# A hybrid decoder step on one core: value tiles turned by VectorE and DMA, copies and loads moved, two buffers for the last blocks

## The chip, the cores and the metric

The kernel runs on one core of one Trainium2 chip. The metric is the device time of one launch in microseconds (us), the median of several runs.

## The reference

One inference step of a one-layer decoder trunk, for 256 prompt tokens and 32 sample tokens (8 sequences of 4), 288 together. Width is 2048, everything is float32.

```
x = x + 1/2 * post1(SwiGLU_1(pre1(x)))
x = x + post2(HybridMixer(pre2(x)))
x = x + 1/2 * post3(SwiGLU_2(pre3(x)))

proj = h @ w_in                                  # q, k, v, a_lr, r | hq, hf, hi, hg
S_t  = diag(exp(log_a_t)) S_{t-1} + k_t^T v_t    # per head, causal
o_t  = q_t S_t                                   # token t reads its own update
out  = concat(rmsnorm(o) * silu(gate)) @ w_out
```

All `pre` and `post` are RMS norms. Each SwiGLU has a hidden width of 5632. The mixer has 4 GLA heads (keys of 128, values of 256) and 8 HGRN heads (128 and 128). The prompt starts with a zero state; each sample sequence brings its own. The outputs are x and the new states.

## The kernel before

**Layout.** Activations lie with features on the 128 partitions and the 288 tokens along the free dimension, in 16 tiles `x[k]` and 16 tiles `y[k]`. Columns 0 to 255 are the prompt, 256 to 287 the samples.

**Matmuls.** A weight unit is 128x1024 numbers, loaded by the SP queue into one of three `raw` buffers (L61, L63). ScalarE rounds it to `wh` (L95) and VectorE makes the remainder `wl` (L96), into one of four buffers. Each product is three matmuls (L520 to L522): `xh*wh`, `xl*wh`, `xh*wl`. A `block` is four output tiles in four PSUM banks of the `mm` pool (five banks): for each k, twelve matmuls, then a call of `tick(k)`. At the block's end `evac(f, ps)` empties each tile. Three more banks are the `aux` pool, for everything else.

**The mixer.** Blocks in order: qk0, v0, qk1, v1, hfq0, hi0, hfq1, hi1, hfq2, hfq3, four gates, then the output projection. A block of values (v0, v1, hi0, hi1) gives four tiles. The scan of a head pair is a generator; every `tick` runs one step of it between two k of a block, and pops one closure from the list `turns` (not at k = 0). The scan's steps 0 to 8 build the causal matrices `Dg` and `Ds` level by level: `put01` places levels 0 and 1 with masked copies (L937, L939, L945, L950), `lay23` prepares the operands of levels 2 and 3 (L976, L977), `score23` multiplies them (L983), `put23` places them (L994). Then `key_t` turns the keys, `out` (L1113 to L1117) multiplies the values by `Dg` and `Ds`, `final` makes the prompt's state (L1126), and `sample` updates and stores the samples' states (L1163, L1165). `load_state` (L895) loads those states, in steps 5 to 8 and on later need.

**Turning the values.** Products come with features on partitions, but the scan's stationary operand needs tokens there. For every tile `ev_v` multiplies by the norm's factor (L849 for the prompt; L850 writes the sample columns three times into `v3`). Its `turn` then makes three PE transposes into one bank (L828 twice, L829) and ScalarE and VectorE copy out the prompt part (`Vt`, L857), the samples (`V32`, L858) and a stacked hi/lo form of the samples (`Vs`, L833 and L835).

**The end.** In the second SwiGLU, x is turned during four earlier output blocks and z (the scaled output) during the last four. `turn32` makes VectorE transposes of 32x32 blocks into `b32` (L625) and `bs32` (L627); after four tiles `move32` moves the blocks to their places by 20 DMAs (L636, L640), for x from POOL, for z alternately from POOL and SP. There is one pair `b32`, `bs32`. The last group of z is turned by PE (`by_token`, L646). `finish` adds and stores.

**Order.** Tile's scheduler lays down each engine's instruction order from the program's order and its own estimate of when operands are ready; `tc.issue_after(ins)` keeps an instruction behind another one on the same engine.

Of the kernel before, what the change touches and what calls it, by code (L numbers as in the profile page):

```python
# [37 lines left out]
class Weights:  # L38


    def __init__(self, tc, rawp, hlp):
        self.tc, self.nc, self.rawp, self.hlp = tc, tc.nc, rawp, hlp
        self.srcs, self.raws, self.parts = [], {}, {}
        self.loaded = self.split = self.used = 0
        self.extra, self.extra_units = None, ()
        self.behind = None
# [8 lines left out]
    def load(self):  # L55
        i, src = self.loaded, self.srcs[self.loaded]
        raw = self.rawp.tile([P, 1024], F32, name=f"raw{i}", tag="raw")
        if isinstance(src, list):
            for c, part in src:
                w = part.shape[2]  # L60
                self.nc.sync.dma_start(raw.rearrange("p (a b) -> p a b", b=512)[:, :, c:c + w], part)  # L61
        else:
            self.nc.sync.dma_start(raw.rearrange("p (a b) -> p a b", b=src.shape[2]), src)  # L63
        self.raws[i] = raw
        self.loaded += 1
# [59 lines left out]
def trunk_kernel(ctx, tc, x_prompt, x_sample, state_gla, state_hgrn, norm_gains, f1_in, f1_out, f2_in, f2_out,  # L125
# [115 lines left out]
    y = [xpool.tile([P, T], F32, name=f"y{k}") for k in range(KT)]  # L241
# [324 lines left out]
    def ffn(tag, gcol, gnext, pn, before, fill=None):  # L566
# [3 lines left out]
        with ExitStack() as pools:  # L570
# [43 lines left out]
            lasts, zs = [], []  # L614

            def last_pool():

                zp = pools.enter_context(tc.tile_pool(name="last", bufs=1, side="right", reuse_waits="tile"))
                for n in ("z", "x"):
                    final_tiles.append((zp.tile([P, KT, 2, P], F32, name=f"{n}T"), zp.tile([P, D // 4], F32, name=f"{n}S")))  # L620

                final_tiles.append((zp.tile([P, 4, 8, TS], F32, name="b32"), zp.tile([P, 4, TS], F32, name="bs32")))

            def turn32(src, f):
                V.transpose(final_tiles[2][0][:, :, 2 * f:2 * f + 2, :],  # L625
                            src[:, 0:TP].rearrange("p (t q c) -> p q t c", t=2, q=4))
                V.transpose(final_tiles[2][1][:, f, :], src[:, TP:T])  # L627

            def move32(g, dst, dsts, queues):

                b32, bs32 = final_tiles[2]
                n = 0
                for b in range(4):
                    rows, cols = slice(b * TS, (b + 1) * TS), slice(b * TS, (b + 1) * TS)
                    for q in range(4):
                        queues[n % len(queues)].dma_start(  # L636
                            dst[q * TS:(q + 1) * TS, 4 * g:4 * g + 4, :, cols].rearrange("p k t c -> p (k t) c"),
                            b32[rows, q])
# [17 lines left out]
            def do_out(c, n):  # L656
# [8 lines left out]
                for o in range(4):  # L665
                    def ev(f, ps):
# [74 lines left out]
    def mixer(pn, border):  # L741
        with ExitStack() as mx:
# [82 lines left out]
            def by_token(tp, src, src3):  # L825

                for t in range(2):
                    PE.transpose(tp[:, t * P:(t + 1) * P], src[:, t * P:(t + 1) * P], ident)  # L828
                PE.transpose(tp[0:96, TP:TP + P], src3, ident)  # L829
# [7 lines left out]
            def vtiles(nm):  # L837
                vs32.append(vs32.pop(0))
                return (gp.tile([P, 2, 512], F32, name=f"V{nm}", tag="V"), vs32[-1],
# [4 lines left out]
            def ev_v(Vt, V32, Vs, y0=8):  # L844
                def ev(f, ps):

                    vt = y[y0 + f]
                    v3 = tmp.tile([P, 3, TS], F32, name="v3", tag="v3", bufs=4)
                    V.tensor_tensor(vt[:, 0:TP], ps[:, 0:TP], rt[:, 0:TP], op=ALU.mult)  # L849
                    V.tensor_tensor(v3, ps[:, TP:T].unsqueeze(1).broadcast_to([P, 3, TS]),  # L850
                                    rt[:, TP:T].unsqueeze(1).broadcast_to([P, 3, TS]), op=ALU.mult)

                    def turn():
                        tp = auxtile("tp_v")
                        by_token(tp, vt, v3.rearrange("p n t -> p (n t)"))
                        c = slice(f * P, (f + 1) * P)
                        S.activation(Vt[:, 0:2, c], tp[:, 0:TP].rearrange("p (t c) -> p t c", c=P), AF.Copy)  # L857
                        S.activation(V32[0:TS, c], tp[0:TS, TP:TP + P], AF.Copy)  # L858
                        stack(Vs[:, c], tp, TS)

                    turns.append(turn)
                return ev
# [9 lines left out]
            def scan(d, Vt, V32, Vs, gla, ytile0, s0, sp_out, ss_out):  # L872
# [56 lines left out]
                def put01(ps, po):  # L929
# [3 lines left out]
                    v = Dflat.rearrange("p (i a) (n two) -> p i a n two", a=2, two=2)  # L933
                    ov = po[:, 0:T].rearrange("p (a c) -> p a c", a=2)
                    sv = Ds[0:TS].rearrange("p a (n two) -> p a n two", two=2)
                    for i in range(2):
                        V.copy_predicated(v[:, i, :, :, 0], eye(P, 64).unsqueeze(1).broadcast_to([P, 2, 64]),  # L937
                                          ov[:, :, i * 64:(i + 1) * 64])
                    V.copy_predicated(sv[:, :, :, 0], eye(TS, 16).unsqueeze(1).broadcast_to([TS, 2, 16]),  # L939
                                      ov[0:TS, :, P:])  # L940
                    for lv in range(2):
                        h = 1 << lv
                        m = mk[:, lv * 64:(lv + 1) * 64]
                        dst = Dflat.rearrange("p j (n two k) -> p j n two k", two=2, k=h)[:, :, :, 1, :]
                        V.copy_predicated(dst, m.rearrange("p (n k) -> p n k", k=h).unsqueeze(1).broadcast_to(dst.shape),  # L945
                                          ps.rearrange("p (j l n k) -> p j l n k", j=4, l=2, k=h)[:, :, lv])
                        dst = Ds[0:TS].rearrange("p a (n two k) -> p a n two k", two=2, k=h)[:, :, :, 1, :]
                        for a in range(2):
                            c = T + a * TS + lv * 16
                            V.copy_predicated(dst[:, a], m[0:TS, 0:16].rearrange("p (n k) -> p n k", k=h),  # L950
                                              po[0:TS, c:c + 16].rearrange("p (n k) -> p n k", k=h))
# [16 lines left out]
                def lay23(part):  # L968
# [7 lines left out]
                    V.tensor_tensor(far, src, f.broadcast_to(src.shape), op=ALU.mult)  # L976
                    S.activation(near, src, AF.Copy)  # L977

                def score23():
                    pss = [auxtile(f"sc23_{i}") for i in range(2)]  # L980
# [61 lines left out]
                for step in range(LEVELS + 1):  # L1042
# [14 lines left out]
                    elif step == 3:  # L1057
                        put01(*pss.pop(1))
                        update(2, False)
                        lay23(1)  # L1060
                    else:
# [7 lines left out]
                        update(step - 1)  # L1069
                    if step == 3:  # L1070
# [35 lines left out]
                def out(a):  # L1106
                    vc = Vt[:, :, a * dv:(a + 1) * dv]

                    po, ss = auxtile("o"), auxtile("os")
                    for j in range(nv):  # L1110
                        vj = vc[:, :, j * P:(j + 1) * P]
# [9 lines left out]
                def final(a):  # L1121

                    kd, vc = kds[a][0], Vt[:, :, a * dv:(a + 1) * dv]
                    ps = auxtile("st")
                    for t in range(2):
                        PE.matmul(ps[:, 0:dv], kd[:, t, :], vc[:, t, :], start=t == 0, stop=t == 1)  # L1126
# [203 lines left out]
            for g in range(2):  # L1330
# [5 lines left out]
                if g == 0:  # L1336
                    vt = vtiles("g0")
                    block("v0", KT, xrhs, ev_v(*vt), 
# [3 lines left out]
                else:  # L1342
                    gla_decay(d, g)
                    vt = vtiles("g1")
                    block("v1", KT, xrhs, ev_v(*vt), tick=tick)
# [3 lines left out]
            for kind, g in HORDER:  # L1349
                if kind == "hi":  # L1350
                    written(g)
                    vts[g] = vtiles(f"h{g}")
                    block(f"hi{g}", KT, xrhs, ev_v(*vts[g], 8 + 4 * g), tick=tick)
# [4 lines left out]
                for j in list(ds):  # L1358
                    if j // 2 in vts:
                        c = slice((j % 2) * 256, (j % 2 + 1) * 256)  # L1360
                        vt, v32, vs = vts[j // 2]
                        gens.append((2 + j, scan(ds.pop(j), vt[:, :, c], v32[:, c], vs[:, c], False, 8 + 2 * j,
# [114 lines left out]
```

## Time and profile before

| | |
|---|---|
| median of 3 runs | 2280.1 us (2279.67 to 2280.32) |
| the profiled execution: time | 2280.79 us |
| its span | 2279.0 us |
| granted TensorE clock, mean | 0.999 |
| busy: PE, DVE, ACT, POOL | 2264.1, 1420.8, 1034.4, 115.8 us |
| DMA | 382.42 MB, mean 168 GB/s |

PE is TensorE, PEld its weight loads, DVE VectorE, ACT ScalarE, POOL GpSimd, SP the sync engine that issues most DMAs. Busy times are shares of the span. Matmuls are pipelined, so the duration of one is longer than the distance to the next one; for what a matmul costs, read the distance between starts. A wait in square brackets in a timeline is idle time before the instruction, with what ended it.

### The profile page before, as it was taken

How to read it: one execution, taken by the hardware profiler on the slowest of the kernel's cores; microseconds unless marked ns; L12 is line 12 of the kernel's file. 1: busy time of each engine (PE TensorE's matmuls, PEld its weight loads, DVE VectorE, ACT ScalarE, POOL GpSimd, SP SyncE). 2: the span in 40 equal slices, each digit the busy share in tenths (PEclk: the TensorE clock that was granted, in tenths of full speed). 3: DMA queues.
4: the chain of work that ended last, by engine and by line, in shares of the span. 5: the costliest groups of instructions: out<-in, count | busy, mean ns of one | idle time of the engine just before them, and what ended most of it. 6: DMA issues, size and time to landing. Idle time of an engine off the chain costs nothing.

```text
span 2279.0 us, 42090 instructions
## 1 busy us (share of the span) xinstructions
PE 2264.1 (99%) x17164; PEld 2252.0 (99%) x17164; DVE 1420.8 (62%) x2375; ACT 1034.4 (45%) x1603; POOL 115.8 (5%) x204
## 2 busy tenths in 40 slices
PE   9999999999999999999999999999999999999998
PEld 9999999999999999999999999999999999999997
DVE  7545545554555468889889754954555455545546
ACT  6443333333334346556656654644333333333344
POOL 0000000000000002001000000260000000000003
PEclk9999999999999999999999999999999999999999
DMA  7555555555555545456465554475555555555555
GB/s 218 169 165 165 165 167 165 166 166 167 167 167 185 166 158 163 139 171 198 144 183 159 167 183 160 141 203 169 165 166 164 166 167 166 167 167 167 167 163 151
DMA packets 228801, 382.42 MB, mean 168 GB/s; under 512 B 24018, under 2 KB 63936, under 8 KB 228608
## 3 DMA queue, kind: packets, MB, share of 16 engines
q1 hardware_dynamic: 219088, 366.27, 50.7%
q0 software_dynamic: 7344, 13.29, 2.1%
q8 instruction: 134, 2.20, 0.4%
q10 hardware_dynamic: 2176, 0.18, 0.1%
q14 instruction: 59, 0.48, 0.1%
HBM read 363.75 MB, written 11.80 MB: 165 GB/s over the span
## 4 chain that ended last, share of the span: by engine, by line
PE 94%; DVE 3%; DMA 1%; ACT 1%; issue 0%; DVEq 0%; SPq 0%; ACTq 0%
PE gate L522 9%; PE gate L520 9%; PE gate L521 9%; PE up L522 8%; PE up L520 8%; PE up L521 8%; PE out L521 8%; PE out L522 8%; PE out L520 8%; PE hfq L520 2%; PE hfq L522 2%; PE mo L522 1%; PE mo L520 1%; PE mo L521 1%; PE hfq L521 1%; PE v L520 1%
## 5 line engine op out<-in xcount | busy, mean ns | idle before, releaser
L96 DVE TENSOR_TENSOR wl<-raw,wh 128x1024 fp32r<-128x1024 f32 (+1 forms) x674 | 821.6, 1219 | 621.0 <-ACT wh L95 619.1
L95 ACT ACTIVATE wh<-raw 128x1024 fp32r<-128x1024 f32 (+1 forms) x674 | 711.6, 1057 | 1017.6 <-PE gate L521 315.8
L522 PE MATMUL gate<-xh,wl 128*128 128x288 f32 x1660 | 489.0, 295 | 0.2 <-DVE wl L96 0.2
L520 PE MATMUL gate<-xh,wh 128*128 128x288 f32 x1660 | 488.9, 296 | 0.3 <-ACT wh L95 0.3
L521 PE MATMUL gate<-xl,wh 128*128 128x288 f32 x1660 | 485.5, 295 | 0.0
L522 PE MATMUL out<-hh,wl 128*128 128x288 f32 x1408 | 415.1, 295 | 0.9 <-DVE wl L96 0.9
L521 PE MATMUL out<-hl,wh 128*128 128x288 f32 x1408 | 415.7, 295 | 0.0
L522 PE MATMUL up<-xh,wl 128*128 128x288 f32 x1408 | 415.0, 295 | 0.0
L520 PE MATMUL up<-xh,wh 128*128 128x288 f32 x1408 | 414.8, 295 | 0.1
L521 PE MATMUL up<-xl,wh 128*128 128x288 f32 x1408 | 414.6, 294 | 0.0
L520 PE MATMUL out<-hh,wh 128*128 128x288 f32 x1408 | 413.7, 294 | 0.0
L522 PEld LDWEIGHTS gate<-xh,wl 128*128 128x128 f32 x1660 | 311.5, 188 | 0.6 <-DVE wl L96 0.6
L520 PEld LDWEIGHTS gate<-xh,wh 128*128 128x128 f32 x1660 | 310.9, 188 | 1.2 <-ACT wh L95 0.5
L521 PEld LDWEIGHTS gate<-xl,wh 128*128 128x128 f32 x1660 | 310.4, 188 | 0.2
L522 PEld LDWEIGHTS out<-hh,wl 128*128 128x128 f32 x1408 | 264.7, 188 | 1.1 <-DVE wl L96 1.1
L520 PEld LDWEIGHTS out<-hh,wh 128*128 128x128 f32 x1408 | 264.6, 188 | 0.0
L520 PEld LDWEIGHTS up<-xh,wh 128*128 128x128 f32 x1408 | 264.1, 188 | 0.5 <-ACT g L590 0.3
L521 PEld LDWEIGHTS out<-hl,wh 128*128 128x128 f32 x1408 | 264.4, 188 | 0.0
L521 PEld LDWEIGHTS up<-xl,wh 128*128 128x128 f32 x1408 | 264.2, 188 | 0.1
L522 PEld LDWEIGHTS up<-xh,wl 128*128 128x128 f32 x1408 | 264.2, 188 | 0.0
L671 DVE TENSOR_TENSOR y<-out,y 128x288 f32<-128x288 f32 x288 | 121.4, 452 | 98.9 <-PE out L522 95.9
L520 PE MATMUL hfq<-xh,wh 128*128 128x288 f32 x256 | 77.5, 303 | 0.0
(381 smaller groups left out, 2598.2 us busy)
## 6 DMA issues: line engine op xcount, KB each, us to landing
raw<-in_ffn_w_in_dram SPq DMA_DIRECT2D x351, 512.0 KB, 3.4
raw<-in_ffn_w_out_dram SPq DMA_DIRECT2D x176, 512.0 KB, 3.5
raw<-in_mix_w_in_dram SPq DMA_DIRECT2D x64, 512.0 KB, 3.7
raw<-in_mix_w_in_dram SPq DMA_DIRECT2D x96, 256.0 KB, 3.2
raw<-in_mix_w_out_dram SPq DMA_DIRECT2D x32, 512.0 KB, 3.7
out_dram<-s POOLq DMA_DIRECT2D x32, 256.0 KB, 3.5
s<-in_state_gla_dram SPq DMA_DIRECT2D x16, 256.0 KB, 4.2
s<-in_state_hgrn_dram SPq DMA_DIRECT2D x16, 256.0 KB, 3.6
```

Source lines behind the costliest of these rows:

```text
L95: i1 = self.nc.scalar.activation(h[:, c], raw[:, c], AF.Copy).ins
L96: i2 = self.nc.vector.tensor_tensor(l[:, c], raw[:, c], h[:, c].bitcast(F32), op=ALU.subtract).ins
L520: yield lambda: PE.matmul(dst, w[0][:, c:c + P], parts[0], start=start, stop=False)
L521: yield lambda: PE.matmul(dst, w[0][:, c:c + P], parts[1], start=False, stop=False)
L522: yield lambda: PE.matmul(dst, w[1][:, c:c + P], parts[0], start=False, stop=stop)
L671: V.tensor_tensor(y[k], ps, y[k], op=ALU.add)
```

## The change

Five edits:

1. `put01` does only the odd masked copies (L945) in step 3 and returns two closures, the even ones and the samples' ones, which run after `lay23`, one in step 3 and one at the end of the next steps. `lay23` issues its ScalarE copy ahead of its VectorE product. The second tile of `score23` comes from the `mm` pool.
2. `load_state` is kept behind the load of the weight unit three before the newest.
3. `b32` and `bs32` have two buffers. For the first two groups of z all moves are issued by POOL; for the third by POOL and SP.
4. `y` is four tiles of four. `ev_v` makes one product of 288 columns. In v0, v1 and hi0 the turns are: two steps of VectorE 32x32 transposes, two tiles a step (the blocks lie in a spare group of `y`), four steps of moves by POOL (16 DMAs of blocks, and with the first step 4 of samples), one empty step. hi1 keeps PE's transposes.
5. In all four blocks the stacked form `Vs` is made from `V32` for four tiles at once (`parts`: two copies of 32x512 on ScalarE, one subtraction on VectorE). `Vt` is laid out by tile, and `out` and `final` index it so.

```diff
-                    pss = [auxtile(f"sc23_{i}") for i in range(2)]
+                    pss = [auxtile("sc23_0"), mmtile("sc23_1")]
...
-                        put01(*pss.pop(1))
+                        puts = put01(*pss.pop(1))
                         update(2, False)
-                        lay23(1)
+                        ready = lay23(1)
+                        with tc.issue_after(ready):
+                            puts.pop(0)()
...
                         update(step - 1)
+                        if puts:
+                            with tc.issue_after(ready):
+                                puts.pop(0)()
...
-                        nc.sync.dma_start(t, s0[b0:b0 + nb, a].rearrange("b p v -> p b v"))
+                        with tc.issue_after(W.last[W.loaded - 3]):
+                            nc.sync.dma_start(t, s0[b0:b0 + nb, a].rearrange("b p v -> p b v"))
...
-                final_tiles.append((zp.tile([P, 4, 8, TS], F32, name="b32"), zp.tile([P, 4, TS], F32, name="bs32")))
+            def blocks32():
+                zp = final_tiles[2]
+                return (zp.tile([P, 4, 8, TS], F32, name="b32", tag="b32", bufs=2),
+                        zp.tile([P, 4, TS], F32, name="bs32", tag="bs32", bufs=2))
...
-                                        move32(o, *zt, (G, nc.sync))
+                                        move32(o, *zt, (G, nc.sync) if o == 2 else (G,))
...
+                def turn32(f):
+                    def run():
+                        for i in (f, f + 1):
+                            V.transpose(b32[:, :, 2 * i:2 * i + 2, :], vg[:, i, 0:TP].rearrange("p (t q c) -> p q t c", t=2, q=4))
+                        if f:
+                            V.transpose(bs32, vg[:, :, TP:T])
+                    return run
+                def move32(b, sample):
+                    rows = cols = slice(b * TS, (b + 1) * TS)
+                    def run():
+                        if sample:
+                            for n in range(4):
+                                r = slice(n * TS, (n + 1) * TS)
+                                G.dma_start(V32[0:TS].rearrange("p (f c) -> p f c", c=P)[:, :, r], bs32[r])
+                        for q in range(4):
+                            G.dma_start(Vt[q * TS:(q + 1) * TS, :, :, cols].rearrange("p f t c -> p (f t) c"), b32[rows, q])
+                    return run
+                def parts():
+                    v = V32[0:TS, :]
+                    S.activation(Vs[0:TS, :], v, AF.Copy)
+                    V.tensor_tensor(Vs[TS:2 * TS, :], v, Vs[0:TS, :].bitcast(F32), op=ALU.subtract)
+                    S.activation(Vs[2 * TS:96, :], v, AF.Copy)
                 def ev(f, ps):
-                    V.tensor_tensor(vt[:, 0:TP], ps[:, 0:TP], rt[:, 0:TP], op=ALU.mult)
-                    V.tensor_tensor(v3, ps[:, TP:T].unsqueeze(1).broadcast_to([P, 3, TS]),
-                                    rt[:, TP:T].unsqueeze(1).broadcast_to([P, 3, TS]), op=ALU.mult)
-                        by_token(tp, vt, v3.rearrange("p n t -> p (n t)"))
-                        stack(Vs[:, c], tp, TS)
+                    V.tensor_tensor(vg[:, f, :], ps, rt, op=ALU.mult)
+                    if spare is None:
+                        turns.append(by_engine(f))
+                    if f == 3:
+                        if spare is not None:
+                            turns.append(turn32(0))
+                            turns.append(turn32(2))
+                            turns.extend(move32(b, b == 0) for b in range(4))
+                            turns.append(lambda: None)
+                        turns.append(parts)
...
-                    block(f"hi{g}", KT, xrhs, ev_v(*vts[g], 8 + 4 * g), tick=tick)
+                    block(f"hi{g}", KT, xrhs, ev_v(*vts[g], 2 + g, None if g else 3), tick=tick)
```

(`ev_v` of v0 and v1 is called with group 2 and spare group 1.)

More of the change, by code (lines that the diff above doesn't have):

```diff
@@ L44, in __init__ @@
         self.loaded = self.split = self.used = 0
+        self.last = {}
         self.extra, self.extra_units = None, ()
@@ L60, in load @@
                 w = part.shape[2]
-                self.nc.sync.dma_start(raw.rearrange("p (a b) -> p a b", b=512)[:, :, c:c + w], part)
+                self.last[self.loaded] = self.nc.sync.dma_start(raw.rearrange("p (a b) -> p a b", b=512)[:, :, c:c + w], part).ins
         else:
-            self.nc.sync.dma_start(raw.rearrange("p (a b) -> p a b", b=src.shape[2]), src)
+            self.last[self.loaded] = self.nc.sync.dma_start(raw.rearrange("p (a b) -> p a b", b=src.shape[2]), src).ins
         self.raws[i] = raw
@@ L240, in trunk_kernel @@
     x = [xpool.tile([P, T], F32, name=f"x{k}") for k in range(KT)]
-    y = [xpool.tile([P, T], F32, name=f"y{k}") for k in range(KT)]
+    yg = [xpool.tile([P, 4, T], F32, name=f"y{k}") for k in range(4)]
+    y = [yg[k // 4][:, k % 4, :] for k in range(KT)]
     xh = [xpool.tile([P, T], F32R, name=f"xh{k}") for k in range(KT)]
@@ L931, in eye @@
                         return mk[0:n, 448:448 + 2 * m].rearrange("p (n two) -> p n two", two=2)[:, :, 0]
[L933 to L951, printed above, removed]
+                    def odd():
+                        for lv in range(2):
+                            h = 1 << lv
+                            m = mk[:, lv * 64:(lv + 1) * 64]
+                            dst = Dflat.rearrange("p j (n two k) -> p j n two k", two=2, k=h)[:, :, :, 1, :]
+                            V.copy_predicated(dst, m.rearrange("p (n k) -> p n k", k=h).unsqueeze(1).broadcast_to(dst.shape),
+                                              ps.rearrange("p (j l n k) -> p j l n k", j=4, l=2, k=h)[:, :, lv])
```

76 lines of the change are left out of this document (52 added, 24 removed).

## The prediction

> **What bounds the kernel now.** I read the page first: busy shares, then the chain that ended last.
>
> ```profile
> PE 2264.1 (99%) x17164; PEld 2252.0 (99%) x17164; DVE 1420.8 (62%) x2375; ACT 1034.4 (45%) x1603; POOL 115.8 (5%) x204
> ...
> PE 94%; DVE 3%; DMA 1%; ACT 1%; issue 0%; DVEq 0%; SPq 0%; ACTq 0%
> ```
>
> TensorE (PE) is busy for 2264.1 of 2279.0 us and the chain is 94% PE. So there are two ways to shorten this kernel: give PE less to do, or take away one of the few moments when it stands still. Whatever the change does to VectorE (DVE), ScalarE (ACT), POOL or the queues counts only where PE comes to wait for it. The windows view says how near the mixer is to that:
>
> ```profile
> 950.00:985.00 35.00, 35.00 (x270) 34.72 (x269) 28.42 (x58) 22.06 (x51) 6.49 (x10) 1.00 0.66 199
> ...
> 1057.00:1093.00 36.00, 35.59 (x286) 34.07 (x285) 30.82 (x84) 18.92 (x49) 2.06 (x3) 1.00 0.52 153
> ```
>
> The columns are PE, PEld, DVE, ACT, POOL, clock, DMA share, GB/s. DVE is busy 28.42 of 35 and 30.82 of 36 us, 81% and 86%: loaded but not full. ACT, POOL and the DMA engines have room. The granted clock is 1.00, so nothing is to be had there.
>
> **Part 1: twelve turned tiles leave PE.** Before, each of the 16 tiles of values is turned by three PE transposes (L828 twice, L829). The change does this for 4 tiles only (block hi1) and turns 12 (blocks v0, v1, hi0) with VectorE and DMAs. What a turn costs PE is not its busy time, since matmuls overlap; it is what it adds between the starts of its neighbours. The timeline of PE at one turn:
>
> ```profile
> 917.81 0.29 PE L522 MATMUL qk<-xh,wl 128*128 128x288 f32 x1
> 917.94 0.38 PE L828 MATMUL tp_v<-ident,y 128*128 128x128 f32 x2
> 918.16 0.27 PE L829 MATMUL tp_v<-ident,v 128*96 128x128 f32 x1
> 918.19 0.38 PE L520 MATMUL qk<-xh,wh 128*128 128x288 f32 x1
> 918.40 0.30 PE L521 MATMUL qk<-xl,wh 128*128 128x288 f32 x1
> 918.54 0.29 PE L522 MATMUL qk<-xh,wl 128*128 128x288 f32 x1
> ...
> 919.87 0.27 PE L828 MATMUL tp_v<-ident,y 128*128 128x128 f32 x1
> ```
>
> Ordinary matmuls start 0.13 us apart (917.81 to 917.94). From 917.81 to 918.54 there are three of them, which would take 0.40, and the turn: 0.73 - 0.40 = 0.33 us. Twelve turns are **4.0 us**. All of it is on the path, since PE does not wait here. The turns of hi1 cost the same as before: their third transpose still streams the 128 columns of the identity.
>
> [...]
>
> **What part 1 adds elsewhere**, from the groups by form:
>
> ```profile
> L625 DVE STREAM_TRANSPOSE b<-x 128x256 f32<-128x256 f32 x16 | 6.5, 414 | 0.1
> L627 DVE STREAM_TRANSPOSE bs<-x 128x32 f32<-128x32 f32 x16 | 2.9, 185 | 0.0
> L835 DVE TENSOR_TENSOR Vsg<-tp_v,Vsg 32x128 fp32r<-32x128 f32 x8 | 2.3, 284 | 0.8 <-ACT Vsg L833 0.6
> L850 DVE TENSOR_TENSOR v<-v,rt 128x96 f32<-128x96 f32 x8 | 2.0, 246 | 0.0
> L96 DVE TENSOR_TENSOR wl<-raw,wh 128x512 fp32r<-128x512 f32 x4 | 2.8, 688 | 0.2 <-ACT wh L95 0.2
> ...
> L857 ACT ACTIVATE Vg<-tp_v 128x256 f32<-128x256 f32 x8 | 3.0, 370 | 0.3 <-PE tp_v L829 0.2
> L858 ACT ACTIVATE vs<-tp_v 32x128 f32<-32x128 f32 x16 | 4.0, 251 | 0.0
> L833 ACT ACTIVATE Vsg<-tp_v 96x128 fp32r<-96x128 f32 x8 | 2.0, 252 | 0.0
> L654 ACT ACTIVATE zS<-tp_s 32x512 f32<-32x512 f32 x1 | 0.6, 585 | 0.1
> ```
>
> DVE, per turned block of four tiles: four block transposes (1.66 us) and one of 128x128, which lies between the 185 and 414 ns rows (take 0.26), come in: 1.92, in three blocks 5.8. In all four blocks one subtraction over 32x512 (bounded by the 688 ns row) replaces four of 284 ns, and the separate 128x96 product (246) goes, while the main one grows by 32 columns (688/512 x 32 = 0.04): about 4 x (0.69 - 1.14 - 0.98 + 0.16) = -5.1. Net +0.7 us over some 400 us of mixer: nothing at 81 to 86% load. ACT loses 16 x 0.252 + 12 x (0.370 + 0.251) = 11.5 and gains 8 copies of 0.585 = 4.7: 6.8 us less.
>
> POOL takes 20 DMAs a block (16 of blocks, 4 of samples). Their nearest rows are the moves of the residual x, which have the same shape:
>
> ```profile
> L636 POOL DMA_DIRECT2D xT<-b x64 | 37.2, 588 | 209.6 <-ACT sq L364 179.1 <-DVE bs L627 27.4 <-DMA xS<-bs 1.2
> L1165 POOL DMA_DIRECT2D out_dram<-s x32 | 23.5, 735 | 62.5 <-DVE s L1163 54.8 <-DMA raw<-in_mix_w_in_dram 5.2 <-DVE k_h L1326 1.9
> ...
> xT<-b POOLq DMA_DIRECT2D x64, 32.0 KB, 3.7
> ```
>
> 20 x 0.588 = 11.8 us of issuing, then 3.7 to land. The first product of values is `out` (L1113); the timeline has it for v0, v1 and hi0, and the start of v1's first turn:
>
> ```profile
> 948.30 0.27 PE L1113 MATMUL o<-Dg,Vg 128*128 128x128 f32 x1
> 986.12 0.38 PE L828 MATMUL tp_v<-ident,y 128*128 128x128 f32 x2
> 1016.74 0.27 PE L1113 MATMUL o<-Dg,Vg 128*128 128x128 f32 x1
> 1084.80 0.28 PE L1113 MATMUL o<-Dg,Vh 128*128 128x128 f32 x1
> ```
>
> The turns start at 917.94, 986.12 and (quoted below) 1058.08, so the values have 30.4, 30.6 and 26.7 us. Needed are two steps for VectorE's four transposes (2 x 1.93, the pitch of turns above), 11.8 and 3.7: 19.4. The slack of 11, 11 and 7 us covers it. Queued behind the moves on POOL are stores of states, which nobody on PE waits for. PE must now look at many DMA semaphores before each first `out`; no row of PE shows that, so it costs between 0 (its sequencer is ahead) and about 0.5 us each, half of the longest wait of PE below. I take 0.2 each, +0.6.
>
> **Part 2: three waits of PE**, each with the row before it:
>
> ```profile
> 931.87 0.29 PE L522 MATMUL qk<-xh,wl 128*128 128x288 f32 x1
> 932.85 0.40 PE L983 MATMUL sc<-R,k_g 128*128 128x192 f32 x1 [0.70 <-DVE R L976]
> ...
> 1057.44 0.29 PE L522 MATMUL hi<-xh,wl 128*128 128x288 f32 x1
> 1058.08 0.33 PE L828 MATMUL tp_v<-ident,y 128*128 128x128 f32 x1 [0.34 <-DVE y L849]
> ...
> 2259.10 0.29 PE L521 MATMUL out<-hl,wh 128*128 128x288 f32 x1
> 2260.29 0.40 PE L522 MATMUL out<-hh,wl 128*128 128x288 f32 x1 [0.90 <-DVE wl L96]
> ```
>
> Less one pitch of 0.13 they are 0.85, 0.51 and 1.06 us.
>
> The first is `score23` waiting for L976, which stands on DVE behind all masked copies of `put01`:
>
> ```profile
> 929.46 0.74 DVE L945 COPY_PREDICATED Dg<-mk,sc 128x256 f32<-128x256 uint8 x1
> ...
> 932.28 0.42 DVE L976 TENSOR_TENSOR R<-Q,F 128x256 f32<-128x256 f32 x1
> ```
>
> 2.8 us lie between those starts. They hold two L945 copies, two products the size of L976 (0.42) and seven smaller copies. With the L945 at 0.54 (pipelined) to 0.74 the seven have 0.5 to 0.9. The change keeps the two L945 there and moves the seven behind L976 and into later steps, so the wait shrinks by 0.5 to 0.85: **0.7**. The second sub-tile of `score23` now takes the fifth matmul buffer instead of an auxiliary one; that can hurt only if a block begins meanwhile, and the scan reaches it amid a block. I price it 0, at most one wait like this one.
>
> The second wait is the first turn of hi0, which PE no longer does: **0.51**.
>
> The third is at the end, where the timelines of SP and DVE show the cause:
>
> ```profile
> 2244.64 6.87 SPq L636 DMA_DIRECT2D zT<-b  x8
> 2251.62 1.05 SPq L63 DMA_DIRECT2D raw<-in_ffn_w_out_dram  x2
> 2259.06 5.19 SPq L636 DMA_DIRECT2D zT<-b  x8
> ...
> 2242.87 0.21 DVE L627 STREAM_TRANSPOSE bs<-z 128x32 f32<-128x32 f32 x1 [0.86 <-DMA zS<-bs]
> 2254.09 0.77 DVE L625 STREAM_TRANSPOSE b<-z 128x256 f32<-128x256 f32 x2 [1.25 <-DMA zS<-bs]
> ```
>
> SP issues the last two weight loads only at 2251.62, after eight moves of z (6.87 us), and DVE waits for the block buffer that earlier moves still read. With two buffers DVE finds one free, and with the first two groups of z on POOL alone SP is open for the weights. POOL then needs 11.8 us a group against 14.4 between groups (2244.64 to 2259.06 by SP), so it keeps up. **1.06** goes.
>
> Later state loads change an order on SP in which no wait of PE is due to a state: 0.
>
> **Sum:** 4.0 + 0.7 + 0.5 + 1.1 - 0.6 = 5.7 us. The profiled execution took 2280.79 (span 2279.0 and 1.8 around it), 0.7 above the median of 2280.1. So the span becomes 2273.3, that execution 2275.1 and the median 2274.4. A difference of 0.2% (4.6 us) is about what a measurement of this kernel can tell from no change.
>
> **Rivals.** *The wait comes back with the moved values.* Engines run in a fixed order laid down beforehand, and the copies of samples on ACT (`parts`) or `out` on PE may stand earlier than their DMAs land (3.7 us after issue). ACT is free to wait, but what queues behind it includes the scan's evacuations. Against it: the slack above. One wait like the longest of the three, 1.06, in each of the three blocks is 3.2: 2277.6. Chance 0.20.
>
> *POOL is held up by DVE.* The 60 issues compete with a VectorE that is over 80% busy. If an issue took f times 0.588, hi0's values come late from f = 1.6 (7.3 of 11.8) and the others from 1.95; at f = 2 PE would lose 4.5 + 0.8 + 0.6 = 5.9 us, just more than the gain, so from there on it is slower; at 2.5 it is 10.4 + 6.7 + 6.5 = 23.6: 2298.0. Against it: L1165 issues in the mixer beside that same DVE in 0.735 us for a transfer eight times as large. [...] Chance 0.07.
>
> *The end is not mended* because the last `wl` is late for another reason, VectorE's own queue: 2275.5. Chance 0.10.
>
> *DVE becomes the bound in the mixer*, so that PE's 4.0 us turn into waits for `wl`, and only the end gains: 2279.0. For it, the 86%; against it, no wait of PE for `wl` there. Chance 0.08.
>
> **Numbers.** The forecast has 0.55, the rivals in their order 0.20, 0.07, 0.10 and 0.08. The range 2272.4 to 2279.5 takes in a gain larger by 2 (0.6 if nothing is lost at `out`, 0.2 if L983's wait goes whole, and one more wait of 1.06 gone with ACT's lighter load), and above it the wait that comes back, the unmended end and the bound on DVE; it leaves out POOL held up. Faster by over 0.2% means under 2275.5: the forecast and half-mended ends, 0.64. Slower by over 0.2% means over 2284.7: 0.08. The rest is 0.28.
>
> **What would show it.** With tp_v, 8 of 32 L828 and 4 of 16 L829 are left. PE's wait list without L983 on R and without L522 on wl at the end; SP's last weight loads before 2245. POOL's new moves near 0.59 us each. Wrong would be: idle time before L1113 or `os`, ACT idle before the samples' copies with a DMA as releaser, or new waits for `wl` in the mixer.

## The result and the profile after

| | before | after |
|---|---|---|
| median | 2279.8 us (20 runs, 2279.04 to 2281.11) | 2282.92 us (20 runs, 2281.28 to 2284.41) |
| the profiled execution: time, span | 2280.79, 2279.0 us | 2282.52, 2280.7 us |
| granted TensorE clock, mean | 0.999 | 0.997 |

The ratio is 1.0013, 95% interval 1.0007 to 1.0019. The changed kernel is 3.1 us slower. A gain of 5.7 us was forecast.

The page of the changed kernel has PE less busy than before, in a longer span:

```profile
PE 2261.5 (99%) x17128; PEld 2250.1 (99%) x17128; DVE 1420.4 (62%) x2362; ACT 1032.9 (45%) x1571; POOL 157.6 (7%) x280
...
PE 95%; DVE 1%; DMA 1%; issue 1%; ACT 1%; POOL 1%; SPq 0%; DVEq 0%; ACTq 0%; POOLq 0%
```

2.6 us less of PE's work and 1.7 us more of span mean that PE stands still longer. The list of PE's waits after the change names the places (columns: what waits, for what, us in total, times, longest):

```profile
PE sc L1041 <- ACT R L1034: 4.4, 1, 4.4
PE sc L1075 <- DVE k_g L1022: 2.4, 2, 1.2
PE warm L296 <- POOL onesD L228: 1.1, 1, 1.1
PE sc L1041 <- DVE R L1035: 0.4, 1, 0.4
```

Lines are those of the changed kernel. L1041 is `score23` (before L983), L1034 the ScalarE copy `near` in `lay23` (before L977), L1035 the product `far`, L1075 the score of a later level, L1022 the product of the keys in `update`. None of the top two stood in the list of before. The wait at the end of the kernel (L522 on `wl`) is gone. SP's timeline there shows why:

```profile
2235.31 13.08 SPq L64 DMA_DIRECT2D raw<-in_ffn_w_out_dram  x5
2259.65 2.71 SPq L645 DMA_DIRECT2D zT<-b  x4
```

The weight loads run on without moves of z between them.

**Where the time went.** I compared the starts of the same block matmuls in the two traces. Up to hi0's scan the changed kernel gets 4.4 us ahead. 1.3 of them come before the first turned tile, and 1.0 of these is a wait that the profiled execution of before had for itself (last section). At one place, in the block hfq1, the changed kernel loses 7.1; at the end it gains 1.2. These sum to a loss of 1.5 us; the spans differ by 1.7. PE's timeline at that place:

```profile
1065.40 0.29 PE L524 MATMUL hfq<-xh,wl 128*128 128x288 f32 x1
1070.13 2.93 PE L1041 MATMUL sc<-R,k_h 128*128 128x192 f32 x8 [4.44 <-ACT R L1034]
1072.60 0.69 PE L522 MATMUL hfq<-xh,wh 128*128 128x288 f32 x1
1073.10 0.44 PE L523 MATMUL hfq<-xl,wh 128*128 128x288 f32 x1
1073.34 0.44 PE L524 MATMUL hfq<-xh,wl 128*128 128x288 f32 x1
```

Two things happen. PE has nothing to start from 1065.53 (one pitch of 0.13 behind the last start, 1065.40) to 1070.13: 4.6 us. And what follows is slow: matmuls start 0.24 us apart where 0.13 is usual. ScalarE's timeline shows what the score waited for:

```profile
1062.36 0.42 ACT L1029 ACTIVATE R<-Q 128x256 f32<-128x256 f32 x1 [0.87 <-PE sc_o L972]
1067.08 0.63 ACT L893 ACTIVATE Vsh<-vs 32x512 fp32r<-32x512 f32 x1 [4.29 <-DMA vs<-y]
1067.61 0.44 ACT L1141 ACTIVATE acc<-k_h 128x96 f32<-128x96 f32 x2
1068.06 0.63 ACT L895 ACTIVATE Vsh<-vs 32x512 fp32r<-32x512 f32 x1
1068.71 1.06 ACT L96 ACTIVATE wh<-raw 128x1024 fp32r<-128x1024 f32 x1
1069.67 0.40 ACT L1034 ACTIVATE R<-Q 128x256 f32<-128x256 f32 x1
```

L893 is the first copy of `parts` for hi0. It stands on ScalarE ahead of L1034 and waits 4.29 us for the DMA that moves hi0's samples; the copy that `score23` needs stands behind it, with four more instructions between them. These are DVE's transposes and POOL's moves of the samples (L886), from the timelines of those engines:

```profile
1055.85 1.42 DVE L874 STREAM_TRANSPOSE y<-y 128x256 f32<-128x256 f32 x4
1057.19 0.27 DVE L876 STREAM_TRANSPOSE y<-y 128x128 f32<-128x128 f32 x1
...
1058.48 1.65 POOL L886 DMA_DIRECT2D vs<-y  x3
1061.71 0.57 POOL L886 DMA_DIRECT2D vs<-y  x1 [1.59 <-issue]
```

The fourth move is issued at 1061.71 and ScalarE goes on at 1067.08, 5.4 us later. The slow stretch is seen when the windows view is cut where the recorded clock changes (columns: PE, PEld, DVE, ACT, POOL, clock, DMA share, GB/s):

```profile
1064.58:1067.99 3.41, 1.11 (x9) 0.88 (x7) 0.25 (x1) 0.92 (x3) 2.31 (x5) 1.00 1.04 244
1067.99:1071.40 3.41, 1.27 (x4) 1.27 (x5) 3.09 (x5) 3.27 (x8) 3.17 (x6) 0.50 0.34 61
1071.40:1074.82 3.42, 3.42 (x15) 3.42 (x14) 1.99 (x7) 0.00 (x0) 0.86 (x2) 0.50 0.83 214
1074.82:1078.23 3.41, 3.41 (x30) 3.25 (x29) 3.09 (x16) 1.06 (x1) 0.00 (x0) 1.00 0.17 45
```

The granted clock is 0.50 from 1067.99 to 1074.82. PE starts again at 1070.13 and works 4.7 us at half speed, which by that clock costs an estimated 2.3 us. Wait and slow clock together are 6.9 of the 7.1 us.

### The profile page after: what moved, and what is told of

It reads as the page before. It is cut to its first block, busy times and chain, and to the rows that moved or that the text cites. A ratio compares the mean times of both kernels' runs of the same rounds, so it can differ in the third digit from the quotient of the medians.

```text
span 2280.7 us, 42039 instructions
## 1 busy us (share of the span) xinstructions
PE 2261.5 (99%) x17128; PEld 2250.1 (99%) x17128; DVE 1420.4 (62%) x2362; ACT 1032.9 (45%) x1571; POOL 157.6 (7%) x280
## 4 chain that ended last, share of the span: by engine, by line
PE 95%; DVE 1%; DMA 1%; issue 1%; ACT 1%; POOL 1%; SPq 0%; DVEq 0%; ACTq 0%; POOLq 0%
PE gate L524 10%; PE gate L522 10%; PE gate L523 10%; PE up L524 8%; PE up L522 8%; PE up L523 8%; PE out L523 8%; PE out L524 8%; PE out L522 8%; PE mo L524 1%; PE mo L522 1%; PE mo L523 1%; PE hfq L522 1%; PE hfq L524 1%; PE hfq L523 1%
## 5 line engine op out<-in xcount | busy, mean ns | idle before, releaser
L96 ACT ACTIVATE wh<-raw 128x1024 fp32r<-128x1024 f32 (+1 forms) x674 | 711.5, 1056 | 1007.8 <-PE gate L523 315.1
L522 PE MATMUL gate<-xh,wh 128*128 128x288 f32 x1660 | 488.8, 296 | 0.0
L522 PE MATMUL up<-xh,wh 128*128 128x288 f32 x1408 | 414.8, 295 | 0.0
L522 PE MATMUL out<-hh,wh 128*128 128x288 f32 x1408 | 413.7, 294 | 0.0
L522 PEld LDWEIGHTS gate<-xh,wh 128*128 128x128 f32 x1660 | 310.9, 188 | 0.7 <-DVE u L600 0.2
L522 PEld LDWEIGHTS out<-hh,wh 128*128 128x128 f32 x1408 | 264.6, 188 | 0.0
L522 PEld LDWEIGHTS up<-xh,wh 128*128 128x128 f32 x1408 | 264.1, 188 | 0.2
L522 PE MATMUL hfq<-xh,wh 128*128 128x288 f32 x256 | 78.3, 306 | 0.0
```

Source lines behind the costliest of these rows:

```text
L96: i1 = self.nc.scalar.activation(h[:, c], raw[:, c], AF.Copy).ins
L522: yield lambda: PE.matmul(dst, w[0][:, c:c + P], parts[0], start=start, stop=False)
```

## The experiments

My theory: ScalarE's copy of the samples stands too early in its order, and the idle time halves the clock. The rivals: the later state loads (edit 2) crowd the DMA engines or ScalarE; the spread copies (edit 1) hold VectorE; the turning itself is worth less than forecast. Each kernel was run beside the kernel before on the same chip; the medians of before in the four groups were 2279.89 (e1 to e4), 2279.62 (e5 to e8), 2279.85 (e9 to e12) and 2280.12 us (e13, e14). Kernels are the changed one with the edit shown, unless said otherwise. The expectations of e9, e10, e13 and e14 number two edits otherwise than the list of the change: what they call edit 3 is the turning (4, with 5), what they call edit 4 the two buffers (3). The 95% interval of each ratio reaches about 2 us to either side, so smaller differences between two kernels are not clear of noise by themselves.

**e1_order: the samples' copies wait behind `near` of the same scan.**

```diff
-                    S.activation(near, src, AF.Copy)
+                    laid[:] = [S.activation(near, src, AF.Copy).ins]
...
+                    with tc.issue_after(laid[0]):
                         S.activation(Vs[0:TS, :], v, AF.Copy)
```

> The changed kernel, with one order added: ScalarE's copies of the sample values (parts) stand behind lay23's copy of the same step sequence. Theory A (the loss is one event: in hi0's scan ScalarE stands 4.3 us before those copies, TensorE waits 4.7 us for lay23's copy behind them, and then runs 6.8 us at half clock): the wait and the low clock go, 4.6 + 2.3 = 6.9 us, so about 2276.0. Theory B (the moves land late because the DMA engines are full at that time, and whatever needs them waits in its turn): the wait moves on to a later product and the time stays within 1.5 us of 2282.9.

Measured: 2278.15 us, ratio 0.9991 (0.9983 to 1.0). 4.8 us came back, and the clock was 1.00 in all of the mixer. But 2.1 us of the wait on R stayed. ScalarE's timeline of this kernel (lines are one higher):

```profile
1066.32 0.42 ACT L1204 ACTIVATE hl<-s 128x256 fp32r<-128x256 f32 x1 [2.63 <-DMA s<-in_state_hgrn_dram]
1066.65 1.04 ACT L96 ACTIVATE wh<-raw 128x1024 fp32r<-128x1024 f32 x1
1067.59 0.40 ACT L1035 ACTIVATE R<-Q 128x256 f32<-128x256 f32 x1
```

With the samples out of the way, a copy of a loaded state stands ahead of `near` and waits for its load: edit 2.

**e2_hi0_pe: hi0 turned by PE again.**

```diff
-ev_v(*vts[g], 2 + g, None if g else 3)
+ev_v(*vts[g], 2 + g, None)
```

> The changed kernel with hi0 turned by TensorE again; v0 and v1 stay with VectorE and DMA. Theory A: the event in hi0 goes (6.9 us) and four turns of 0.33 and the first-turn wait of about 0.5 come back: 2277.8. If VectorE and DMA turns cost as much in v0 and v1 as in hi0 (theory C: turning by moves is dear everywhere): 2280 or more.

Measured: 2278.14 us, ratio 0.9992 (0.9983 to 1.0001). The wait on R and the low clock are gone. In the changed kernel the loss hangs on hi0 alone; v0 and v1 have none there.

**e3_loads: edit 2 undone.**

```diff
-                        with tc.issue_after(W.last[W.loaded - 3]):
-                            nc.sync.dma_start(t, ...)
+                        nc.sync.dma_start(t, ...)
```

> The changed kernel without the delay of the state loads (edit 2 undone). Theory A with the state loads as what makes the samples late (three state loads are issued within 4 us of the samples' moves in the changed kernel, one in the kernel before): the moves land 3.7 instead of 5.2 us after issue, the stand of ScalarE shrinks to 1 to 2 us, the clock stays up, and the time is 2276 to 2278. If the weights alone fill the DMA engines there: no change, 2282.9.

Measured: 2281.63 us, ratio 1.0008 (0.9999 to 1.0017). The wait on R is 3.8 us instead of 4.4 and the clock is 0.50 for 3.41 instead of 6.83 us. The state loads are not the main cause.

**e4_filled: 40 products that nothing reads ahead of hi0's `score23`.**

```diff
+                    if not gla and ytile0 == 8:
+                        for _ in range(40):
+                            PE.matmul(pss[0][:, 384:512], onesD, onesD, ...)
```

> The changed kernel with 40 extra products of constants (0.109 us each, 4.4 us, results unused) put on TensorE ahead of hi0's score23, where it otherwise stands idle for 4.7 us. Theory A with the clock falling because TensorE was idle: the wait is filled, the clock stays at full, and the 2.3 us of slow matmuls go: 2280.6. If the low clock has another cause, or its cost is already inside the wait: 2282.9 or, if the extra products delay what follows, up to 2287.

Measured: 2284.34 us, ratio 1.002 (1.0011 to 1.0029). The clock stayed at 1.00, but I had taken too many products:

```profile
1066.03 9.09 PE L1041 MATMUL sc<-onesD 128*128 128x128 f32 x80
1074.96 1.47 PE L1044 MATMUL sc<-R,k_h 128*128 128x192 f32 x8
1076.13 0.43 PE L522 MATMUL hfq<-xh,wh 128*128 128x288 f32 x1
```

They took 9.09 us where 4.6 were idle: each of these products is two matmuls in the trace (x80), and 0.11 us was the pitch of one matmul. One number is good: `score23` now takes 1.17 us to the next block matmul, against 2.47 (1070.13 to 1072.60) in the changed kernel. The half clock cost 1.30 us there, and about 1.0 on the eight matmuls behind it, which agrees with the 2.3 above.

**e7_fill18: the same with 18 products.**

> After, with 18 idle products of 128x128 float32 ahead of hi0's score: e4_filled's 40 took 9.09 us, so 18 take 4.1 us, about the time for which TensorE waited there (4.73 us), and TensorE does not stand idle. Theory A: the granted clock then stays at 1.00, and the 4.7 us that ran at half clock after the wait lose nothing: 2282.9 - 2.35 = 2280.6 us. Rival B: the low clock is only recorded, or came from the load on the DMA engines and not from the idle time: 2282.9 us, or clock 0.5 again in that stretch.

Measured: 2286.56 us, ratio 1.003 (1.0018 to 1.0041): both expectations missed. The 18 products took 4.18 us and the wait on R was gone. But Tile laid down another order on VectorE, and the next score came to wait for its keys:

```profile
1075.96 1.73 PE L1078 MATMUL sc<-Q,k_h 128*112 128x64 f32 x8 [3.25 <-DVE k_h L1022]
...
1068.97:1072.38 3.41, 3.41 (x26) 3.30 (x25) 3.15 (x12) 1.77 (x6) 2.45 (x5) 1.00 0.35 50
1072.38:1075.80 3.42, 0.33 (x3) 0.10 (x1) 3.42 (x13) 1.06 (x1) 0.28 (x1) 1.00 0.77 236
1075.80:1079.21 3.41, 3.25 (x15) 3.28 (x16) 2.44 (x9) 0.00 (x0) 0.00 (x0) 0.50 0.00 0
1079.21:1082.62 3.41, 3.41 (x29) 3.07 (x28) 1.71 (x4) 0.54 (x2) 0.00 (x0) 0.50 0.51 136
```

So this run does not price the clock. It does show the low clock a second time, after another idle stretch with another cause, and with the DMA share at 0.00 in the first window where the clock is low.

**e5_order_loads: e1 with edit 2 undone as well.**

> After, with the parts' copies kept behind the near copy of the same scan as in e1_order, and the state loads issued as before (edit 2 undone). Theory A: what was left in e1_order's wait of the score on R (2.1 us) is ScalarE's copy of a state, which stands ahead of the near copy and waited 2.63 us for its load; with the loads early the copy comes sooner and the wait goes: 2278.15 - 2.1 = 2276.0 us, no wait over 0.5 us of the score on ACT R. Rival B: the near copy is late for another reason (the sampled values, or VectorE), and 2278.2 us stays.

Measured: 2275.77 us, ratio 0.9983 (0.9974 to 0.9992). As theory A had it: no wait on R is left in this scan.

**e6_order_puts: e1 with edit 1 undone**, so edit 2 is in.

```diff
-                        puts = put01(*pss.pop(1))
+                        for f in put01(*pss.pop(1)):
+                            f()
+                        puts = []
...
                         ready = lay23(1)
-                        with tc.issue_after(ready):
-                            puts.pop(0)()
```

> After, with the order of e1_order and edit 1 undone: all masked copies of the first two levels are made in step 3 again. Theory A: the two waits of the scores on the key product (2.4 us together) come from edit 1, which left two later batches of masked copies that VectorE takes ahead of the key product; they go, and the old wait of one score on R (0.85 us) may come back: 2278.15 - 2.4 = 2275.8 us to 2276.6 us. Rival B: these waits come from the turning and its moved values (another order of VectorE's work), and 2278.2 us stays with the waits on k_g in place.

Measured: 2279.83 us, ratio 1.0002 (0.9993 to 1.0011); slower than e1 where I expected faster. The waits on k_g did shrink, from 2.4 to 1.1 us. But waits for states grew: 2.6 us on R, and a new one, here with the row of ScalarE behind it:

```profile
PE sc L1062 <- DVE k_h L1023: 1.6, 1, 1.6
...
1246.22 0.42 ACT L1204 ACTIVATE hl<-s 128x256 fp32r<-128x256 f32 x1 [5.47 <-DMA s<-in_state_hgrn_dram]
```

ScalarE stood 5.47 us before a copy of a state whose load edit 2 had put off. A rounding of weights (L96) queued behind it, and VectorE, in order, waited for that ahead of the keys.

**e8_three: e5, and the later masked copies kept behind the key product of their step.**

```diff
-                        update(step - 1)
+                        ready = update(step - 1)     # now returns its key product
                         if puts:
                             with tc.issue_after(ready):
```

> After, with the order of e1_order, the state loads as before, and the two later batches of masked copies kept behind the key product of their step (not behind the far product of step 3). If the three causes add up: 2278.15 - 2.1 (copy of the state) - 2.4 (key product) = 2273.7 us, and no wait of a score over 0.7 us in the scans. Rival: the copies that now come later make the waits of the next levels' scores or of the reads of D, and 2275.5 us or more is left.

Measured: 2275.19 us, ratio 0.9981 (0.9973 to 0.999); between the two. The waits on k_g went from 1.2 to 0.2 us, a wait on k_h of 0.5 us and others of 0.2 to 0.4 came. What made the wait in the changed kernel is seen in VectorE's timeline, with PE's row last:

```profile
930.91 0.44 DVE L992 COPY_PREDICATED Dg<-mk,sc_o 128x128 f32<-128x128 uint8 x1
931.15 1.25 DVE L97 TENSOR_TENSOR wl<-raw,wh 128x1024 fp32r<-128x1024 f32 x1
932.32 0.43 DVE L992 COPY_PREDICATED Dg<-mk,sc_o 128x128 f32<-128x128 uint8 x1
932.55 0.33 DVE L1052 COPY_PREDICATED Dg<-mk,sc 128x128 f32<-128x128 uint8 x1
932.78 0.41 DVE L1022 TENSOR_TENSOR k_g<-k_g,F 128x256 f32<-128x256 f32 x1
...
933.87 0.97 PE L1075 MATMUL sc<-Q,k_g 128*112 128x64 f32 x8 [1.21 <-DVE k_g L1022]
```

The moved even copies (L992), a weight remainder and a copy of `put23` all stand ahead of the key product.

**e9_end_only: the kernel before with edit 3 alone.**

> Before with edit 4 alone: two block buffers for z, the first two groups of z on POOL's queue only. If the last weight loads are what held TensorE at the end, the 1.06 us wait goes there and nothing changes elsewhere: 2279.7 - 1.1 = 2278.6 us, and the idle time at the last block is under 0.2 us. If the last wait is VectorE's own, 2279.7 us stays.

Measured: 2278.84 us, ratio 0.9997 (0.9988 to 1.0006), 1.0 us under before. PE has no wait at the last block, whose start is 1.17 us earlier against the rest.

**e10_no_turns: PE turns all 16 tiles.**

```diff
-ev_v(*vt, 2, 1)
+ev_v(*vt, 2, None)        # v0, v1; and hi0 as in e2
```

> After with edit 3's turning undone for all blocks: TensorE turns all 16 tiles again, the new layout of the values and the other edits stay. e2_hi0_pe (2278.14 us) turned 8 by VectorE. If each of these eight saves TensorE the 0.33 us of the prediction and costs nothing, this is 2278.1 + 2.6 = 2280.8 us. If the two waits of scores on the key product (2.0 us in e2_hi0_pe) come from the turning, they go and 2278.8 us is left.

Measured: 2280.37 us, ratio 1.0003 (0.9994 to 1.0011). Eight turns fewer on PE are worth 2.2 us (to e2), 0.28 each. The waits on k_g are 1.6 us here without any turning, so they are not due to it.

**e11_hi0_pe_loads: e2 with edit 2 undone.**

> After with hi0's values turned by TensorE and the state loads issued as before. Theory A: late state loads hurt only through copies of states that stand ahead of others on ScalarE, 0.6 us in e2_hi0_pe, so 2277.5 us; beside e5_order_loads (2275.8) this makes turning hi0 by VectorE worth 1.8 us (four turns of 0.33 and the 0.5 us wait) once nothing waits for the moves. Rival B: the late loads cost more than the waits on them show, since they move other work: 2276.5 us or less, and turning hi0 is worth under 1 us.

Measured: 2279.32 us, ratio 0.9997 (0.9988 to 1.0006), with runs from 2277.51 to 2280.82. Neither theory: the wait for a state is gone from the trace, whose execution took 2277.51 us as theory A had it, but the median is 1.2 us above e2. I did not find out why this kernel spreads.

**e12_order_loads_puts: e5 with edit 1 undone**, that is edits 3 to 5 with the order of e1.

> e5_order_loads with edit 1 undone as well (all masked copies of the first two levels in step 3 again). As the prediction had it, edit 1 saves 0.7 us at the score on R and costs nothing: 2275.8 + 0.7 = 2276.5 us. The rival: edit 1 itself makes the waits of the scores on the key product (1.2 us in e5_order_loads), so those go and the one on R comes back: 2275.8 - 1.2 + 0.85 = 2275.4 us. The two are close in time; the waits of the trace tell them apart.

Measured: **2274.72 us**, ratio 0.9977 (0.9969 to 0.9986), the fastest kernel of all. The forecast for the whole change was 2274.4; the forecast's terms for edits 3 to 5 alone (4.0, 0.5 and 1.1, less 0.6) sum to 5.0 us, and this kernel is 5.1 under its before. The list of PE's waits:

```profile
PE warm L296 <- POOL onesD L228: 1.1, 1, 1.1
PE sc L1041 <- ACT wh L96: 0.6, 1, 0.6
PE gate L524 <- DVE wl L97: 0.3, 1, 0.3
PE sc L1075 <- DVE k_g L1022: 0.2, 1, 0.2
```

**e13_puts_loads and e14_puts: edits 1 and 2 undone, and edit 1 alone, without the reordering.**

> After with edits 1 and 2 undone and nothing reordered: edits 3 and 4 alone. ScalarE's copy of hi0's samples stands ahead of the near copy of the same scan, as in the changed kernel. Theory A: that place alone makes the wait of the score on ACT R (3.8 to 4.4 us) and the half clock after it; beside e12_order_loads_puts (2274.7), which differs only in that place, that is 2274.7 + 4.8 (what e1_order gained over the changed kernel) = 2279.5 us, 2278.5 to 2281.5. Rival B: the wait needs edit 1's or edit 2's other order of work, and this is within 1.5 us of 2274.7.

> After with edit 1 undone: edits 2, 3 and 4. Both kinds of copies stand ahead of the near copy of hi0's scan on ScalarE, that of the samples and those of states whose loads come late. Theory A: both waits come, the longer one counts first: e6_order_puts (2279.8) + 4.8 = 2284.6 us, with a wait of over 4 us on ACT R and a granted clock of 0.5 after it. Rival B: undoing edit 1 frees VectorE enough to make good for it, 2281.5 us or less.

Measured: 2279.1 us, ratio 0.9993 (0.9985 to 1.0002), and 2282.16 us, ratio 1.0007 (0.9998 to 1.0016). Theory A's wait comes in e13: L893 waits 3.77 us for hi0's samples without edits 1 and 2. But PE's idle time (2.75 us from start to start, less a pitch) lies across two windows of 3.41 us (last section), with 1.74 us idle in one and 0.84 in the next, and the clock stayed at 1.00. By the starts of the block matmuls e13 loses 2.75 us to e12 at this place, and 1.2 and 0.8 us in the scans of v0 and v1, where L893 stands ahead as well and waits 1.51 and 1.86 us for samples. In e14 PE waits 3.1 us on R and the clock fell; the time lies between its two expectations. Side by side in the windows view, two rows of e14 and then two of e13:

```profile
1066.78:1070.20 3.42, 0.32 (x4) 0.09 (x2) 1.28 (x2) 3.38 (x10) 1.71 (x4) 1.00 0.70 151
1070.20:1073.61 3.41, 3.41 (x12) 3.41 (x13) 1.25 (x5) 0.47 (x2) 2.48 (x5) 0.50 0.74 176
...
1066.64:1070.05 3.41, 1.67 (x13) 1.44 (x11) 1.47 (x10) 2.17 (x5) 3.41 (x7) 1.00 0.37 63
1070.05:1073.47 3.42, 2.57 (x17) 2.53 (x17) 2.63 (x7) 1.63 (x3) 2.64 (x5) 1.00 0.47 67
```

**All eight together** (medians, us; edits 3, 4 and 5 in all of them):

| edit 1 | edit 2 | samples' copies as changed | kept behind `near` | gain by order |
|---|---|---|---|---|
| in | in | 2282.92 (after) | 2278.15 (e1) | 4.8 |
| in | out | 2281.63 (e3) | 2275.77 (e5) | 5.9 |
| out | in | 2282.16 (e14) | 2279.83 (e6) | 2.3 |
| out | out | 2279.10 (e13) | 2274.72 (e12) | 4.4 |

The order of the samples' copies is worth 4.3 us on the mean of the four rows. Edit 2 costs 1.3, 3.1, 2.4 and 5.1 us, mean 3.0. Edit 1 costs 0.8, 2.5, -1.7 and 1.1, mean 0.7, which is not clear of zero. The prices differ from row to row, since a wait hides others behind it and every edit lets Tile lay down a new order.

## Why the prediction was wrong

Point by point, by its own steps.

- **Twelve turns leave PE (4.0 us): right in kind.** The shift of the block starts over qk1's four turns is 1.32 us, as forecast; e10 against e2 gives 0.28 a turn, so 3.4 for twelve.
- **POOL's moves: the issue was sized rightly, the slack was not.** POOL took 0.585 us an issue for blocks (48 of them) and 0.555 for samples, forecast 0.588. What failed is the step "The slack of 11, 11 and 7 us covers it". I measured the slack to `out`, the first product that reads values, and in the order of the old trace. The first reader is ScalarE's copy of the samples, and Tile had set it ahead of `near`, which `score23` needs at 1065.5 in the changed kernel, 20.7 us before hi0's first `out` there (1086.24). With the prediction's own sizes, four issues of 0.588 from 1058.48 and 3.7 to land, the samples come at 1064.5; L893 and the four instructions between it and `near` take 2.6 us (1067.08 to 1069.67), so `near` starts at an estimated 1067.1, after the time it is needed. Two things made it later: POOL paused 1.59 us ahead of the fourth move, and that one took 5.4 us instead of 3.7, in a stretch with a DMA share of 1.04.
- **The deadline moved too.** The rows show the last first-level score and `score23` of hi0's scan before, then that first-level score after the change:

```profile
1066.67 0.31 PE L925 MATMUL sc_o<-R,k_h 128*32 128x32 f32 x4
1072.67 0.56 PE L983 MATMUL sc<-R,k_h 128*128 128x192 f32 x2
...
1062.01 0.31 PE L972 MATMUL sc_o<-R,k_h 128*32 128x32 f32 x4
```

  Between the two PE had 41 block matmuls before, and 24 in the changed kernel (34 in e6, e12, e13 and e14, which leave out edit 1). The new order asks for `near` 17 matmuls, an estimated 2.3 us, sooner. By the old order the same sizes leave no wait: moves from 1061.94 (two pitches of 1.93 behind 1058.08) bring the samples at an estimated 1068.0 and `near` at 1070.6, ahead of 1072.67. So what the prediction had wrong is both: which instruction waits first, and that its place in the order would stay.
- **The rival was the right one, and mis-sized.** "The wait comes back with the moved values" names ScalarE's `parts` and what queues behind it. I priced it at 1.06 us in each of three blocks. It came once, in hi0, at 4.6 us, with a slow clock after it that cost 2.3 and that no step had. The mistake in its price is taking the longest wait of the old trace as a bound for a new one: what bounds it is how late the data are.
- **Edit 1's first wait (0.7 us): it went, and another came.** The score no longer waits for `far` in the first scan, but the copies that moved out of the way stand ahead of the next step's key product: 2.4 us in two scans. The prediction followed the moved copies out of one step and not into the next.
- **"Later state loads ... no wait of PE is due to a state: 0": wrong**, 3.0 us on the mean. That nobody waited for states in the old trace said that they came early enough, not that they could come later. A late state held ScalarE (2.63 us in e1, 5.47 in e6), and what PE needed queued behind it.
- **hi0's first turn (0.51): gone**, as forecast. **`out` (+0.6): nothing**; no run shows this term, and no wait of PE at `out` is in the list. **The fifth matmul buffer (0): nothing seen.**
- **The end (1.06): right**, 1.17 in the trace, 1.0 in e9's median. SP's last weight load came at 2248.0 and not before 2245, which was soon enough.

The sum closes: e12, with the three faults out, is 5.1 us under its before (5.7 forecast for the change). Adding edit 1 (0.7), edit 2 (3.0) and the order (4.3) gives 2.9 us over; 3.1 was measured. This is no independent check, since the three prices come from the same eight medians. How the half clock alone counts was read off the trace and e4 but not separated: my attempt, e7, changed VectorE's order too.

## What to carry to other kernels

When work moves to a DMA, take as its deadline the first instruction that waits for it on any engine, and then what stands behind that instruction on the same engine; the consumer that you care about may be another one. A load that no one waits for has slack, and putting it off spends that slack (3.0 us lost on the mean here): look at which engine in order would stand still if it were gone. Where the scheduler lays down the order, keeping a late copy behind an urgent one was worth 4.3 us here, more than the 3.4 to 4.0 that twelve turns took off TensorE. A new order can also bring a deadline forward, as it did for `score23`, so a slack read from the old trace is only an estimate.

## What was not expected of the hardware

**The recorded clock changed in steps of 3.41 us.** It was low for 3.41 us (e3, e14) or twice that (after, e7). In the changed kernel the fall at 1067.99 comes 1204.91 us before the fall at the kernel's end, 2272.90, which is 353 steps of 3.413 us. I laid the windows back by this step from the last fall where a trace has only that one, such as e13's; that they lie so there is my assumption. With those edges, the windows around hi0's `score23` sort themselves in seven traces (after, e1, e3, e6, e7, e13, e14): after 3.41 us in which PE was busy 0.32 (e14), 0.33 (e7), 0.40 (e3), 1.11 or 1.27 us (after) the next were at 0.50, after 1.67 us (e6, e13) or more at full clock they were at 1.00. It is not a firm threshold, as the last two windows of e13 show, where PE's work is transposes and products of one column:

```profile
2264.73:2268.14 3.41, 2.17 (x17) 1.72 (x16) 2.35 (x6) 2.45 (x7) 0.29 (x1) 1.00 0.02 6
2268.14:2271.55 3.41, 0.00 (x0) 0.00 (x0) 3.41 (x7) 0.00 (x0) 0.00 (x0) 0.50 1.04 366
```

There 2.17 us of PE's recorded work were followed by the low clock. By these rows an idle stretch such as e13's 2.75 us could cost more than itself if it lay within one window, which would leave an estimated 0.83 us busy (3.41 less the 1.74 and 0.84 idle); I did not try that. One busy window did not always bring the clock back: e7 had a second one at 0.50 after 3.25 of 3.41 us busy.

**The profiled execution of before has a wait of its own.** PE's list of before has this row:

```profile
PE v L520 <- ACT q_g L1281: 0.7, 1, 0.7
```

The idle time there is 0.99 us longer than in e9, which leaves that part of the kernel as it was. Part of what the two first traces seemed to differ by was that; the profiled execution (2280.79 us) lies 0.99 above the median of before.

**The same pause on POOL** (1.57 to 1.59 us ahead of the fourth move of hi0's samples) stands in all eleven traces in which POOL moves hi0's samples. What makes it I don't know. No run shows POOL's issues held up by VectorE, and none rules it out for this pause, so it is open whether the rival "POOL is held up by DVE" has a part in it.
